# Tile copies on another queue, statistics in pieces, and router logits from the rows before their norm

## The chip, the core and the metric

The kernel runs on one core of one Trainium2 chip. TensorE multiplies matrices and accumulates in PSUM banks of 128 x 512 fp32, VectorE, ScalarE and GpSimd work element by element on SBUF (VectorE and ScalarE on PSUM too), and SyncE and ScalarE issue DMAs from queues of their own. The metric is the device time of one execution in microseconds, the median of several.

## What is computed

256 tokens of 1024 features go through two blocks. The first has two layers, `x = norm(ALPHA*x + mix)` and `x = norm(ALPHA*x + experts(x))`; in layer 0 `mix` is a convolution module, in layer 1 differential attention. The second block (a state-space mixer beside stick-breaking attention, and a feed-forward) is not touched. What the change bears on:

```python
def conformer_conv(x, w_pw1, b_pw1, w_dw, b_dw, g, b, w_pw2, b_pw2):
    a, gate = jnp.split(x @ w_pw1 + b_pw1, 2, axis=-1)
    h = depthwise_conv_31(a * jax.nn.sigmoid(gate), w_dw) + b_dw
    return jax.nn.silu(layer_norm(h, g, b)) @ w_pw2 + b_pw2

def grouped_moe(x, router_w, router_bias, w_gate, w_up, w_down):
    aff = jax.nn.sigmoid(x @ router_w)              # 16 experts in 4 groups
    # best group by the two best of aff + router_bias, then its two best experts
    # gates: aff of the two, over their sum
    out = sum_e gates[:, e] * ((jax.nn.silu(x @ w_gate[e]) * (x @ w_up[e])) @ w_down[e])
```

## The kernel before

The program is written as one straight line; a scheduler orders the instructions of each engine by the program's order, as far as their inputs and buffers are ready by its own model, and puts in the waits. `keep_in_program_order` and `after` (L341) pin single instructions.

Weights come in units of 1 MB in a fixed order (`order`, L283) through rings of SBUF slots: ring1 and ring2 hold 11 units, ring3, ring5 and ring4 another 8 once the convolution's or the attention's buffers are given back. All units are issued from SyncE's queue (`issue`, L317), each when its slot is free. fp32 products are made of three fast ones: a weight half is split in a high part (ScalarE, L367) and a low part (GpSimd or VectorE, L376), and `mm3` (L379) multiplies high by high, low by high and high by low.

`phase_a` (L568) is layer 0's convolution module. For each of 8 tiles of 128 channels the first projection is done on TensorE, ScalarE takes the sigmoid of the gate (`sg`), and VectorE writes the product to `hp` (L650). Channels are then convolved over time with 31 taps. Tiles 0, 1 and 3 are convolved on VectorE, tap by tap into a PSUM bank (L614; `CONV_RUNS` says how many taps follow each gate, and the next gate is pinned behind them). The other five go to TensorE: `shifted` (L596) writes `hp` of a tile to DRAM (`hd`, L603), reads it back four times with a shift (`xq`, L605), and makes a banded weight on GpSimd (L599); `conv` (L618) does 64 matmuls. Two convolutions are called between projections (tiles 5 and 6), three behind them, then `turn` (L626) transposes the result back to tokens by features in four banks, and `normalize` (L423) takes mean and variance (L429) and writes `n`. After silu the second projection `pw2` (`proj_q`, L698) runs over four units; in the last unit the four results (two token blocks by two halves of the features) are finished one after the other, and `done` adds each to the residual `res` (L689).

Then comes the routing, the same in both layers: `norm_rows` (L443) normalizes the residual rows in place; `moe` (L723) copies them as the high part `xnh` (ScalarE, L735), `to_fm` (L446) transposes them to features by tokens, VectorE and ScalarE apply gain and bias (L742, L744), 8 small matmuls in four column groups give the logits `lg` (L749), two more sum the groups (L754), and ScalarE takes the sigmoid `affs` (L756). VectorE makes the low part `xnl` (L759). `route` (L941) sorts on VectorE with some twenty small operations: `sel` (L945), ranks, masks, positions (by TensorE, L959), gates. `gather` (L777) then picks each expert's rows with one-hot matmuls over `xnh` and `xnl` (`px`, L787 and L790), and the experts begin. `warm` (L356) puts matmuls of no use on TensorE where it would stand idle; `W` counts them.

In attention `bias` (L1102) reads each head pair's bias from `vecd`, a DRAM table that holds a row of 384 values 128 times per head, so that one access pattern with a stride of 383 gives the diagonal form.

## Time and profile before

| | us |
|---|---|
| median of three runs (1165.78 to 1167.7) | 1167.34 |
| the profiled execution | 1166.63 |
| its span, first to last instruction | 1164.9 |

| stretch of the span, us | what runs |
|---|---|
| 0 to 89 | projections and convolutions of layer 0 |
| 89 to 119 | norm, silu, second projection |
| 119 to 139 | norm, routing and gather of layer 0 |
| 139 to 346 | experts of layer 0 |
| 346 to 469 | attention |
| 469 to 490 | norm, routing and gather of layer 1 |
| 490 to 697 | experts of layer 1 |
| 697 to 1165 | second block |

A row of a timeline gives the start in us from the span's start, the duration (of several instructions together, x their number), engine, line, operation, output<-inputs, shape, and in brackets how long the engine sat idle before and what ended that. PE is TensorE, DVE VectorE, ACT ScalarE, POOL GpSimd, SPq and ACTq the issuing queues of SyncE and ScalarE. A wait is put down to what came last by the profile. The clock is the mean share of TensorE's full clock that was granted.

### The profile page before, as it was taken

Reading aid. Unit: us, or ns where it says so; the run is one execution under the profiler, and the core shown is the slowest. Engines: PE = TensorE matmul, PEld = TensorE weight load, DVE = VectorE, ACT = ScalarE, POOL = GpSimd, SP = SyncE. Lnnn points to the kernel's source line nnn. Section 1 sums busy time; section 2 is a strip of 40 time slices with the busy share of each in tenths; the row PEclk is TensorE's granted clock in tenths of the full one; section 3 lists DMA queues with packets and bytes.
Section 4 is the critical chain, followed back from the end, with each engine's and each line's share of the span. In section 5 each row is a group of like instructions: output and inputs, shape, how many; then the busy total and the mean of one; then the engine's idle time right before and its main releaser. Section 6 shows DMA issues by size and latency. Waiting matters only on the chain.

```text
span 1164.9 us, 18257 instructions
## 1 busy us (share of the span) xinstructions
PE 1112.4 (95%) x7235; PEld 790.8 (68%) x7235; DVE 631.8 (54%) x1259; ACT 455.3 (39%) x798; POOL 308.1 (26%) x187
## 2 busy tenths in 40 slices
PE   9879989999999998989999999999999999999996
PEld 7857434444337997434344337989999988999996
DVE  6936721232227766721233227866988858665555
ACT  4314311011216665311011116555677566444443
POOL 5922000000003432000000005552324574444443
PEclk9989999999999999999999999999999999999998
DMA  9989489999999645599999993443323452554551
GB/s 358 308 260 403 152 364 418 420 419 421 419 415 415 238 161 218 240 372 387 419 419 421 419 418 106 161 155 118 128 92 109 173 208 73 217 181 167 196 199 55
DMA packets 53215, 315.11 MB, mean 271 GB/s; under 512 B 7111, under 2 KB 13312, under 8 KB 17024
## 3 DMA queue, kind: packets, MB, share of 16 engines
q1 hardware_dynamic: 49016, 309.02, 68.3%
q10 hardware_dynamic: 4104, 4.82, 1.3%
q8 instruction: 60, 0.98, 0.3%
q14 instruction: 35, 0.29, 0.1%
HBM read 312.01 MB, written 3.39 MB: 271 GB/s over the span
## 4 chain that ended last, share of the span: by engine, by line
PE 41%; DVE 9%; ACT 3%; DMA 1%; issue 1%; POOL 0%; ACTq 0%; DVEq 0%; POOLq 0%; SPq 0%
PE up L382 4%; PE up L383 4%; PE py L812 4%; PE up L381 4%; PE pu L812 4%; PE pg L812 3%; DVE E L1548 2%; PE pdn L383 2%; PE pdn L382 2%; PE pdn L381 2%; PE dwin L381 1%; PE dwin L382 1%; PE dwin L383 1%; DVE dwin L1342 1%; PE dwout L383 1%; PE dwout L382 1%
## 5 line engine op out<-in xcount | busy, mean ns | idle before, releaser
L812 PE MATMUL pu<-u_moe,xe 128*64 128x512 f32 x256 | 114.6, 600 | 4.7 <-PEq L991 4.7
L812 PE MATMUL py<-u_moe,hT 128*64 128x512 f32 x256 | 114.0, 596 | 1.4 <-DMA u_moe<-in_moe 0.8
L813 PE MATMUL pu<-u_moe,xe 128*64 128x512 f32 x256 | 114.7, 600 | 0.0
L813 PE MATMUL py<-u_moe,hT 128*64 128x512 f32 x256 | 113.6, 596 | 0.0
L812 PE MATMUL pg<-u_moe,xe 128*64 128x512 f32 x256 | 113.4, 593 | 0.0
L813 PE MATMUL pg<-u_moe,xe 128*64 128x512 f32 x256 | 113.0, 593 | 0.0
L881 DVE TENSOR_TENSOR h<-h,pu 128x512 f32<-128x512 f32 x16 | 11.0, 688 | 184.3 <-PE pu L813 171.6
L381 PE MATMUL dwin<-xih,wh 128*128 128x272 f32 (+1 forms) x352 | 104.8, 298 | 1.1 <-DVE xih L1288 1.1
L382 PE MATMUL dwin<-xil,wh 128*128 128x272 f32 (+1 forms) x352 | 102.1, 290 | 1.1 <-DVE xil L1289 1.1
L382 PE MATMUL up<-fxl,wh 128*128 128x258 f32 (+1 forms) x352 | 100.5, 285 | 1.6 <-DVE fxl L1729 1.6
L383 PE MATMUL dwin<-xih,wl 128*128 128x272 f32 (+1 forms) x352 | 101.5, 288 | 0.0
L381 PE MATMUL up<-fxh,wh 128*128 128x258 f32 (+1 forms) x352 | 100.4, 285 | 0.8 <-ACT fxh L1728 0.8
L383 PE MATMUL up<-fxh,wl 128*128 128x258 f32 (+1 forms) x352 | 100.4, 285 | 0.0
L376 POOL TENSOR_TENSOR wl<-u_win,wh 128x1024 fp32r<-128x1024 f32 x25 | 60.3, 2412 | 62.6 <-ACT wh L367 59.9
L916 DVE SCALAR_TENSOR_TENSOR yl<-py,gc,yh 128x512 fp32r<-128x512 f32 x32 | 24.0, 751 | 94.7 <-ACT yh L915 93.7
L812 PEld LDWEIGHTS pu<-u_moe,xe 128*64 128x64 f32 x256 | 35.1, 138 | 59.2 <-issue 58.0
L812 PEld LDWEIGHTS py<-u_moe,hT 128*64 128x64 f32 x256 | 33.4, 137 | 59.9 <-issue 56.0
L812 PEld LDWEIGHTS pg<-u_moe,xe 128*64 128x64 f32 x256 | 34.6, 137 | 54.7 <-issue 53.6
L376 POOL TENSOR_TENSOR wl<-u_wup,wh 128x1024 fp32r<-128x1024 f32 x22 | 52.8, 2401 | 64.7 <-ACT wh L367 64.7
L382 PEld LDWEIGHTS up<-fxl,wh 128*128 128x128 f32 x352 | 67.7, 192 | 2.5 <-DVE fxl L1729 1.8
L381 PEld LDWEIGHTS up<-fxh,wh 128*128 128x128 f32 x352 | 67.6, 192 | 2.0 <-ACT fxh L1728 1.3
L382 PEld LDWEIGHTS dwin<-xil,wh 128*128 128x128 f32 x352 | 67.0, 190 | 2.0 <-DVE xil L1289 1.9
(526 smaller groups left out, 3025.6 us busy)
## 6 DMA issues: line engine op xcount, KB each, us to landing
u_moe<-in_moe SPq DMA_DIRECT2D x192, 1024.0 KB, 18.6
u_win<-in_win SPq DMA_DIRECT2D x22, 1024.0 KB, 4.9
u_wup<-in_wup SPq DMA_DIRECT2D x22, 1024.0 KB, 5.3
u_pw<-in_pw SPq DMA_DIRECT2D x11, 1024.0 KB, 11.6
u_wdown<-in_wdown SPq DMA_DIRECT2D x11, 1024.0 KB, 4.9
u_wout<-in_wout SPq DMA_DIRECT2D x8, 1024.0 KB, 4.9
u_wk<-in_wk SPq DMA_DIRECT2D x4, 1024.0 KB, 15.8
u_wq<-in_wq SPq DMA_DIRECT2D x4, 1024.0 KB, 16.2
```

The costliest lines, as they stand in the source:

```text
L376: eng.tensor_tensor(l, w, h.bitcast(F32), ALU.subtract)
L381: mm(ps, lh, rh, start=first, stop=False)
L382: mm(ps, lh, rl, start=False, stop=False)
L383: mm(ps, ll, rh, start=False, stop=last)
L812: nc.tensor.matmul(ps[0:64], a, ra, start=first, stop=last)
L813: self.upped = nc.tensor.matmul(ps[64:128], b, rb, start=first, stop=last)
L881: nc.vector.tensor_tensor(h, h, pu, ALU.mult)
L916: nc.vector.scalar_tensor_tensor(yl[:, s], py[nh], gc, yh[:, s].bitcast(F32), op0=ALU.mult, op1=ALU.subtract)
L1342: nc.vector.scalar_tensor_tensor(pb, raw[:, k:k + L], wc(k), pb, op0=ALU.mult, op1=ALU.add)
L1548: nc.vector.tensor_scalar(E[:, q:q + w], a[:, i, q:q + w], nA[:, c, h:h + 1], 0.0, op0=ALU.add, op1=ALU.min)
```

## The change

In the convolution: `hd` is written from ScalarE's queue; there are four `xq` buffers for three; one convolution lies between projections (behind tile 6) and four behind them; the tiles are transposed in the order of `TURN`, in three goes between the convolutions, and the statistics are taken in four pieces per token block. `vecd` holds 32 copies for 128, made one projection earlier, and each bias load becomes four DMAs of 32 partitions.

In the routing: gain, bias and mean are taken out of the logits. With r = 1/std and m = mean of a row, `(x - m)*r*g @ w + b @ w` is `r*(x @ (g*w)) - m*r*(g @ w) + b @ w`. `router` makes `g*w` and the two constants of each expert early in stage A. `Head.done`, behind each finished quarter of the residual, adds it, takes its statistics, and transposes the quarter before it as it is, not normalized; ScalarE copies that to `xr`. `last` does the logits from `xr`, and `gates` applies r and m to the 16 logits of a row. The rows are normalized behind that (`rows`), one block on VectorE, one on GpSimd, and GpSimd makes the low part in four pieces.

```diff
-W = dict(start=16, a=16, l0=16, lg=9, pos=(4, 6), f0=22, f1=22, l1=18, mix=20)
+W = dict(start=16, a=13, head=(1, 2), lg=13, pos=(4, 6), f0=22, f1=22, mix=20)
+TURN = (0, 1, 2, 4, 5, 6, 3, 7)
+VCOPY = 32
+class Head:
+    def turn(self, tb, nh):
+        bank = self.net.bank(f"rt{self.l}{tb}{nh}")
+        s = slice(nh * 512, nh * 512 + 512)
+        for j in range(4):
+            self.nc.tensor.transpose(bank[:, j * P:(j + 1) * P], self.res[tb][:, (4 * nh + j) * P:(4 * nh + j + 1) * P], self.net.ident)
+        self.nc.scalar.activation(self.xr[tb][:, s], bank, AF.Copy)
+    def done(self, tb, nh, pp):
+        x = self.res[tb][:, nh * 512:nh * 512 + 512]
+        nc.vector.tensor_tensor(x, pp, x, ALU.add)
+        nc.vector.bn_stats(self.st[tb][:, nh], x)
+        if nh:
+            nc.vector.bn_aggr(self.mv[:, tb], self.st[tb])
+        if self.due:
+            self.turn(*self.due)
+        self.due = (tb, nh)
+    def last(self):
+        self.lg = net.bank(f"lg{l}")
+        self.logits(0, range(KT))
+        net.warm(W["head"][0])
+        self.turn(*self.due)
+        nc.vector.tensor_scalar(v, self.mv[:, :, 1], LN_EPS, None, op0=ALU.add)
+        self.r = net.rsqrt_act(v, [P, TB], f"l{l}")
+        nc.vector.scalar_tensor_tensor(self.nmr, self.mv[:, :, 0], -1.0, self.r, op0=ALU.mult, op1=ALU.mult)
+        self.logits(1, range(4))
+        net.warm(W["head"][1])
+        self.logits(1, range(4, KT))
+    def gates(self, b1):
+        nc.scalar.activation(lgs, self.lg[:, :T], AF.Copy)
+        net.preload(AF.Sigmoid)
+        for tb in range(TB):
+            nc.tensor.matmul(pa[:, tb * NE:(tb + 1) * NE], lgs[:, tb * P:(tb + 1) * P], net.col("groups", 0, NE), start=True, stop=True)
+        for tb in range(TB):
+            nc.vector.scalar_tensor_tensor(lin[:, tb], net.cd[:, l, 0], self.nmr[:, tb:tb + 1], net.cd[:, l, 1], op0=ALU.mult, op1=ALU.add)
+        for tb in range(TB):
+            self.lin = nc.vector.scalar_tensor_tensor(lin[:, tb], pa[:, tb * NE:(tb + 1) * NE], self.r[:, tb:tb + 1], lin[:, tb], op0=ALU.mult, op1=ALU.add)
+        nc.scalar.activation(aff, lin, AF.Sigmoid)
+    def rows(self, xnh, xnl):
+        for tb in range(TB):
+            i = (nc.gpsimd if tb else nc.vector).tensor_scalar(self.res[tb], self.res[tb], self.mv[:, tb, 0:1], self.r[:, tb:tb + 1], op0=ALU.subtract, op1=ALU.mult)
+            if not tb:
+                self.net.after(i, self.lin)
+            self.net.tc.keep_in_program_order(nc.scalar.activation(xnh[tb], self.res[tb], AF.Copy))
+        for h in range(2):
+            s = slice(512 * h, 512 * h + 512)
+            for tb in range(TB):
+                i = nc.gpsimd.tensor_tensor(xnl[tb][:, s], self.res[tb][:, s], xnh[tb][:, s].bitcast(F32), ALU.subtract)
...
-        self.vecd = self.dram.tile([NH, P, 384], F32, name="vecd")
+        self.vecd = self.dram.tile([NH, VCOPY, 384], F32, name="vecd")
...
-        self.pe3 = self.pool(early, "pae3", 3)
+        self.pe3 = self.pool(early, "pae3", 4)
...
-            self.load(hd, hp[:, j])
+            nc.scalar.dma_start(hd, hp[:, j])
...
+        def moments(c):
+            for tb in range(TB):
+                nc.vector.bn_stats(stats[tb][:, c], halves[tb][c // 2][:, c % 2 * 256:c % 2 * 256 + 256])
...
-            if j in (0, 1, 4):
+            if j in (0, 1, 3):
                 next(rel_bias, None)
-            if j in (5, 6):
+            if j in (2, 3, 5):
+                next(router, None)
+            if j == 6:
                 conv()
...
-        while conv_in:
-            conv()
-        for i in range(2):
-            turn(i)
+        conv()
+        conv()
+        turn(0, 1, 2, 3)
+        conv()
+        turn(4, 5)
+        for c in range(3):
+            moments(c)
+        conv()
+        turn(6, 7)
+        moments(3)
...
+            for i in range(P // VCOPY):
+                nc.scalar.dma_start(bt[VCOPY * i:VCOPY * i + VCOPY], ...)
```

## Rows read from the trace of the kernel before

**Rows 1.** The page: busy time, share of the span and instructions of each engine.
```profile
PE 1112.4 (95%) x7235; PEld 790.8 (68%) x7235; DVE 631.8 (54%) x1259; ACT 455.3 (39%) x798; POOL 308.1 (26%) x187
```
**Rows 2.** Windows: length, busy PE PEld DVE ACT POOL, clock, DMA share, GB/s.
```profile
79.10:83.50 4.40, 0.00 (x0) 0.00 (x0) 0.00 (x0) 0.44 (x1) 0.00 (x0) 1.00 1.07 242
83.60:88.90 5.30, 5.30 (x65) 2.94 (x66) 0.00 (x0) 0.00 (x0) 0.00 (x0) 0.68 1.01 418
...
130.00:140.00 10.00, 8.98 (x55) 5.51 (x55) 7.67 (x29) 3.32 (x5) 0.00 (x0) 1.00 0.01 3
140.00:160.00 20.00, 19.25 (x92) 6.84 (x90) 5.20 (x11) 1.09 (x3) 0.00 (x0) 1.00 0.89 354
```
**Rows 3.** Waits of TensorE from 50 to 90 us: total, times, longest.
```profile
PE cv L623 <- DMA xq<-hd: 10.5, 3, 4.8
```
**Rows 4.** Waits of SyncE's queue over the whole span.
```profile
SPq L275 <- DMA hd<-hp: 25.5, 5, 10.7
```
**Rows 5.** Timeline of SyncE's queue: start, duration, what is issued.
```profile
64.73 0.38 SPq L275 DMA_DIRECT2D hd<-hp  x1
...
72.55 0.34 SPq L275 DMA_DIRECT2D hd<-hp  x1
...
75.44 1.75 SPq L275 DMA_DIRECT2D xq<-hd  x4
```
**Rows 6.** Timeline of TensorE: last convolutions, then the routing of layer 0.
```profile
59.33 3.25 PE L623 MATMUL cv<-xq,band 128*32 128x256 f32 x29 [4.78 <-DMA xq<-hd]
...
75.35 3.66 PE L623 MATMUL cv<-xq,band 128*32 128x256 f32 x64 [1.15 <-DMA xq<-hd]
83.56 5.33 PE L623 MATMUL cv<-xq,band 128*32 128x256 f32 x64 [4.55 <-DMA xq<-hd]
...
118.58 0.39 PE L383 MATMUL pw<-wh,sl 128*128 128x512 f32 x1
...
122.73 2.16 PE L452 MATMUL fm_x1T<-cst_m,res 128*128 128x128 f32 x16 [0.26 <-DVE res L440]
...
133.80 0.36 PE L787 MATMUL px<-S,nh 128*128 128x256 f32 x1
```
**Rows 7.** Timeline of VectorE: taps, the first norm, the routing of layer 0.
```profile
57.46 9.41 DVE L614 SCALAR_TENSOR_TENSOR conv<-hp,cols_a,conv 128x256 f32<-128x256 f32 x18
...
72.03 0.48 DVE L650 SCALAR_TENSOR_TENSOR hp<-pw,cols_a,sg 128x256 f32<-128x256 f32 x1 [2.00 <-ACT sg L649]
...
92.29 0.17 DVE L432 TENSOR_SCALAR v_a<-mv_a 128x2 f32<-128x2 f32 x1
...
129.91 0.19 DVE L945 TENSOR_TENSOR sel<-affs,row_router_b 128x32 f32<-128x32 f32 x1 [1.94 <-ACT affs L756]
```
**Rows 8.** DMAs that write or read tile xq: issue to landing.
```profile
DMA to landing us min/median/max: 3.5/6.1/10.2
```
**Rows 9.** Groups by line and form, 118 to 131 us: busy, mean ns, idle before.
```profile
L759 DVE TENSOR_TENSOR nl<-res,nh 128x1024 fp32r<-128x1024 f32 x2 | 2.4, 1216 | 0.0
...
L735 ACT ACTIVATE nh<-res 128x1024 fp32r<-128x1024 f32 x2 | 2.0, 1040 | 0.0
...
L440 DVE TENSOR_SCALAR res<-res,mv_l,y_l 128x512 f32<-128x512 f32 x2 | 1.0, 542 | 0.0
```
**Rows 10.** Groups of GpSimd over the whole span: the nearest prices.
```profile
L1818 POOL TENSOR_TENSOR o<-o,hm 128x512 f32<-128x512 f32 x3 | 3.7, 1260 | 9.0 <-DVE o L1817 9.0
...
L762 POOL CAST idg<-cst_m 128x256 fp32r<-128x256 f32 x2 | 0.8, 396 | 17.7 <-PE wo L383 10.3 <-PE pw L383 7.4
```
**Rows 11.** Timelines of GpSimd and VectorE in attention: two small operations in a row.
```profile
404.59 2.43 POOL L376 TENSOR_TENSOR wl<-u_wv,wh 128x1024 fp32r<-128x1024 f32 x1 [7.03 <-ACT wh L367]
...
404.61 2.43 DVE L419 SCALAR_TENSOR_TENSOR t_sub<-t_sub,ss 128x4 f32<-128x4 f32 x1
407.07 0.16 DVE L420 SCALAR_TENSOR_TENSOR y_sub<-t_sub,y_sub 128x4 f32<-128x4 f32 x1
```
**Rows 12.** Timeline of ScalarE's queue in attention.
```profile
401.96 0.38 ACTq L1104 DMA_DIRECT2D bt<-vecd  x1
```

More of the change, by code (lines that the diff above doesn't have):

```diff
@@ L426, in normalize @@
         for tb in range(TB):
-            st = self.tiny.tile([P, 2, 6], F32, tag="bnst", name=f"st_{name}{tb}")
-            for i in range(2):
-                nc.vector.bn_stats(st[:, i], src[tb][i])
+            if stats:
+                st = stats[tb]
+            else:
+                st = self.tiny.tile([P, 2, 6], F32, tag="bnst", name=f"st_{name}{tb}")
+                for i in range(2):
+                    nc.vector.bn_stats(st[:, i], src[tb][i])
             nc.vector.bn_aggr(mv[:, tb], st)
@@ L485, in build @@
             c3 = ExitStack()
-            xs = self.phase_a(late, early, c3) if "A" in phases else self.skip("n1", c3)
-            for i in range(TB):
-                self.dump(f"n1{i}", xs[i])
+            xs, head = self.phase_a(late, early, c3)
             rows = lambda l: self.rows.get(l) or self.mix_rows(l)
             if "B" in phases:
-                xs, src = self.moe(0, xs, "mix_g0", "mix_b0", ["ring4", "ring5", "ring3"], rows(0))
+                xs, src = self.moe(0, xs, head, "mix_g0", "mix_b0", ["ring4", "ring5", "ring3"], rows(0))
             else:
@@ L498, in build @@
             self.retire = {}
-            xs = self.attention(xs, c3) if "C" in phases else self.skip("n3", c3)
-            for i in range(TB):
-                self.dump(f"n3{i}", xs[i])
+            xs, head = self.attention(xs, c3)
             if "D" in phases:
-                xs, src = self.moe(1, xs, "mix_g1", "mix_b1", ["ring4", "ring5", "ring3", "ring2"], rows(1))
+                xs, src = self.moe(1, xs, head, "mix_g1", "mix_b1", ["ring4", "ring5", "ring3", "ring2"], rows(1))
             else:
@@ L555, in rel_bias, with router @@
         yield
-        self.vecd = self.dram.tile([NH, P, 384], F32, name="vecd")
-        self.load(self.vecd, bass.AP(tensor=vecs.tensor, offset=vecs.offset, ap=[[384, NH], [0, P], [1, 384]]))
+        self.vecd = self.dram.tile([NH, VCOPY, 384], F32, name="vecd")
+        self.load(self.vecd, bass.AP(tensor=vecs.tensor, offset=vecs.offset, ap=[[384, NH], [0, VCOPY], [1, 384]]))
+    def router(self, pool, pin):
+        nc = self.nc
+        cols = self.held["cols_m"]
+        at = COL_AT["mix_g0"][1]
+        affine = cols[:, at:at + 8 * KT].rearrange("p (l c k) -> p l c k", l=DEPTH, c=4)
+        self.gw = self.yy.tile([P, DEPTH, (KT + 1) * NE], F32, name="gw")
+        nc.gpsimd.memset(self.gw[:, :, KT * NE:], 0.0)
+        for l in range(DEPTH):
+            self.after(nc.gpsimd.tensor_tensor(self.gw[:, l, :KT * NE].rearrange("p (k e) -> p k e", e=NE), self.col("router_w", 0, KT * NE).rearrange("p (k e) -> p k e", e=NE),
+                                    affine[:, l, 0].unsqueeze(2).to_broadcast([P, KT, NE]), ALU.mult), pin())
+        yield
+        pc = self.bank("cd")
+        for k in range(KT):
+            r = slice(32 * (k % 4), 32 * (k % 4) + 32)
+            nc.tensor.matmul(pc[r, :4], self.col("router_w", NE * k, 32), affine[:, :, 0:2, k], start=k < 4, stop=k >= 4)
+        part = pool.tile([P, 4], F32, name="cd_part")
+        nc.scalar.activation(part, pc[:, :4], AF.Copy)
+        yield
+        both = pool.tile([P, 384], F32, tag="rb_oh", name="ones_m")
+        ones, spread = both[:, :P], both[:, P:P + 4 * NE].rearrange("p (c e) -> p c e", c=4)
+        self.after(nc.gpsimd.memset(ones, 1.0), pin())
+        nc.gpsimd.tensor_tensor(spread, self.col("groups", 0, NE).unsqueeze(1).to_broadcast([P, 4, NE]), part.unsqueeze(2).to_broadcast([P, 4, NE]), ALU.mult)
+        pd = self.bank("cds")
+        nc.tensor.matmul(pd[:, :4 * NE], ones, spread.rearrange("p c e -> p (c e)"), start=True, stop=True)
+        self.cd = self.yy.tile([P, DEPTH, 2, NE], F32, name="cd")
+        nc.scalar.activation(self.cd.rearrange("p l c e -> p (l c e)"), pd[:, :4 * NE], AF.Copy)
     def open_a(self, late, early):
@@ L634, in phase_a @@
         rel_bias = self.rel_bias(e1)
+        router = self.router(e1, lambda: glu)
         res = [self.act.tile([P, D], F32, tag=f"xacc{tb}", name=f"res{tb}") for tb in range(TB)]
@@ L666, in phase_a @@
         self.preload("natural_log_exp_and_others")
-        while conv_in:
-            conv()
-        for i in range(2):
-            turn(i)
+        conv()
[8 more added lines that the diff above has]
+        moments(3)
         self.dump("convy", y)
         self.warm(W["a"])
-        self.normalize(halves, n, "a", AF.Silu)
+        self.normalize(halves, n, "a", AF.Silu, stats)
         early.close()
@@ L721, in mix_rows, with moe @@
         return [self.row(f"mix_{c}{l}", self.yy, t, late) for c, t in (("g", "yh"), ("b", "yl"))]
[L723 removed]
+    def moe(self, l, n, head, gname, bname, last_rings, rows):
         nc = self.nc
```

88 lines of the change are left out of this document (46 added, 42 removed).

## The prediction

> **What bounds the kernel now.** First the page: TensorE is busy 95% of the span and the other engines at most 68% [rows 1]. So time can only be saved where TensorE waits or works slowly, or where it runs for nothing. The second thing to look for is what the DMA does in those places, because the two expert stages load 96 MB each and a start of the experts that comes earlier is worth nothing if their weights do not come earlier too.
>
> The windows show both. In front of the first expert stage the DMA stands still: it moves 3 GB/s from 130 to 140 us, while TensorE is in the routing, and 354 GB/s from 140 to 160 us [rows 2]; in front of the second the same stretch is there again (two in all). The rings are full there, and the next slot comes free when the first experts have used a unit. So an expert stage that begins x us earlier restarts the stream x us earlier, and what is saved up to the end of a routing goes through to the end of the kernel one to one, as long as x is less than the standing time (10 us or more). What follows behind the experts is not touched by the change.
>
> The change touches three stretches that are in series with everything else:
> - the depthwise convolution and the norm behind it. TensorE waits 10.5 us in three pieces for the shifted copies xq [rows 3], and because it stood idle from 79.1 to 83.5 us it does the last convolution at a mean clock of 0.68 [rows 2], that is between the two levels of 1.2 and 2.4 GHz: 5.33 us where the same 64 matmuls took 3.66 us [rows 6];
> - the routing of layer 0, from the last matmul of the projection (its start at 118.58 plus 0.39 is 118.97 us; I call this end E) to the first matmul of the gather at 133.80 us: 14.8 us [rows 6];
> - the same routing in layer 1.
>
> **Stage A, part by part.** A tile's way is: VectorE writes hp, SyncE copies it to DRAM (hd), waits for the landing, loads xq from it, TensorE convolves. SyncE does this in order, and it waited 25.5 us for five landings of hd, once 10.7 us [rows 4]. So the copy of tile 6 went out at 64.73 us [rows 5], though VectorE had finished that tile's hp before it began the taps at 57.46 us [rows 7]: over 7 us lost in the queue alone. The change issues hd from ScalarE's queue, and each xq can be loaded as soon as its own hd has landed.
>
> The second thing is the order on TensorE. The last gate (hp of tile 7) was ready at 72.03 us because TensorE came to tile 7's projection only after the wait for tile 4's copy. Now only one convolution lies between projections. Tile 6's projection ended at 59.33 - 4.78 = 54.5 us, where the wait for tile 4 began [rows 6], with one convolution (3.66 us) ahead of it that now follows it, so tile 7's projection (5.9 us) runs from about 54.5 to 60.4 us, and its gate waits only for the 18 taps that precede it in VectorE's order: 57.46 + 9.41 + 0.48 = 67.4 us [rows 7], 5.1 us earlier than now.
>
> From there: ScalarE issues hd in 0.4 us, landing 2.5 us (72.55 to 75.44 now, less the issue [rows 5]), so xq of tile 7 is issued at 70.3 us. Now it took from 75.44 to 83.56 us to arrive [rows 5, 6], 8.1 us; landing times of all twenty pieces lie between 3.5 and 10.2 us with 6.1 in the middle [rows 8]. I take 7.2 us, between 6.1 and 8.1: 77.5 us. TensorE is there before: 60.4 + three convolutions of 3.7 + twelve transposes at 0.135 (16 took 2.16 us [rows 6]) + 1 us for the new router matmuls = 74.1 us. It idles 3.4 us, so I leave the last convolution at its slow 5.33 us: end at 82.9 us. Behind it come ScalarE's copy (0.5), the last 4 transposes (0.7 with latency), two short statistics (0.8) and the rest (0.6): v_a at 85.5 us against 92.29 us [rows 7]. **Gain 6.8 us, I say 7.** Bounds: with xq in 4.8 us (3.5 plus the other issues) and full clock 10.9 us; with 11.5 us for xq 2.6 us. The smaller DRAM copy vecd (0.4 MB for 1.5 MB) is inside these bounds.
>
> What pays: hd on ScalarE's queue makes ScalarE wait for VectorE's gate. Behind it in order stand the weight split of tile 7 and the sigmoid of the gate. For tile 6 this can hold ScalarE up to 57.5 us, and tile 7's projection would end at 66 us rather than 60.4, still below 67.4; then TensorE reaches the last convolution at 80 us and the gain is about 6, within the bounds. GpSimd gets about 1.2 us of small router work; it has slack once the bands of later tiles wait for their buffers.
>
> **The routing, per layer.** Removed from the path: the write of the normalized rows, 16 transposes behind it (2.16 us [rows 6]), the affine copies. Added ahead of E: three groups of four transposes on TensorE between projection matmuls, 12 x 0.135 = 1.6 us, uncovered. So E moves to E' = E + 1.6. From E', with durations of the same operations in layer 0: addition and statistics to the variance 1.9 us, then Ln behind the last copy of the turned sums (0.3 late), Ln, Exp and three small operations: r at E' + 3.3. Meanwhile the logits: last turn at E' + 1.0 to 1.5, ScalarE's copy to 2.3, last logits to 2.9, copy to 3.3, sums over groups to E' + 3.9. So the scalars and the logits come out together, and VectorE can put them together (four small operations) by E' + 4.4 at the best.
>
> Then the new costs. GpSimd normalizes one row block at r, and this is a form that the trace doesn't have; the nearest is a cast of 256 columns in 396 ns, so 1.6 us for 1024, and above it the two-input 1024 columns in 2.43 us [rows 10, 11]. Does it hold VectorE up? In attention a VectorE operation on 128x4 that normally takes 0.16 us took 2.43 us, exactly as long as GpSimd's operation beside it [rows 11]. So I take 1.2 us for this: the four operations end at E' + 5.6. VectorE's own row block follows (two halves of 542 ns [rows 9], 1.1 us) and only then sel: E' + 6.75. From sel to the gather it is 133.80 - 129.91 = 3.9 us as now [rows 6, 7]. Sum: E + 1.6 + 6.75 + 3.9 = E + 12.25 for E + 14.8 now, **gain 2.6 us**.
>
> Last, the low halves xnl. They lay on VectorE, 2.4 us behind the affine copies while the logits were under way [rows 9], and move to GpSimd, four operations on 128x512 at 1.26 us [rows 10]. They can start 1.15 us behind sel (ScalarE's copy xnh, 1.04 us [rows 9]), so they lie beside the sorting operations on VectorE, which wait for nothing else. If none is held the cost is 0; if each of the four holds one operation, 4 x 1.0 = 4.0 us. I take 1.4 us: the reductions and the operations that read PSUM need not be held, and of the small operations in attention only those that began under a running GpSimd operation were. **Gain 1.2 us per layer**, bounds +3.8 (nothing held, VectorE's combination at 4.4) and -2.2 (2.43 for 1.6, and 4.0).
>
> The Trainium skill has a rule on this, in "SBUF — State Buffer", section "Who interferes with whom": a VectorE instruction with two SBUF inputs and a GpSimd instruction that reads SBUF share one port pair under an exclusive lock, and the second one blocks for the whole of the first. By it the low halves would take the whole 4.0 us and a layer would lose 1.4 us instead of gaining 1.2; rows 11 agree with it, the other operations of this chain were never seen beside GpSimd.
>
> **Attention.** The bias loads become 16 issues for 4. One issue is 0.38 us of ScalarE's queue [rows 12]; three more, at two places inside softmax, are 1.2 us each time. TensorE has projections to do beside softmax, so I count 0.3 us in all; uncovered it is 2.4 us.
>
> **Sum.** The profiled execution took 1166.63 us (span 1164.9), 0.7 us below the median of the three, within their spread. 1166.6 - 7.0 - 2 x 1.2 + 0.3 = **1157.5 us**.
>
> **Rivals.**
> - Nothing is held: GpSimd's operations fall into gaps of VectorE's chain. For it: half of the sorting chain are reductions and PSUM reads. 1166.6 - 7 - 7.6 + 0.3 = 1152.3 us.
> - The copies don't come earlier: hd leaves from another queue but over the same DMA engines, which are full (share 1.07 from 79.1 to 83.5 us [rows 2]), and xq stays behind 1 MB loads in SyncE's queue. Then only the lower bound of stage A, 2.6 us: 1161.9 us. "DMA: Bandwidth & Descriptors" of the Trainium skill, section "Issuing engines are not separate DMA queues", speaks for this one: another issuing engine saves only the issue time. By that alone stage A would gain next to nothing and the sum would be about 1164 us; the wait of SyncE for landings [rows 4] speaks against it.
> - Slower: the lock in each routing. GpSimd's 2.43 us and all four low halves stand between VectorE's operations (E + 18.1, a loss of 3.3 us), and TensorE, which has then nothing to do for over 6 us, drops to the lower level as at 83.6 us [rows 2] and loses about 1.9 us on the gather: 5.2 us per layer. 1166.6 - 7 + 10.4 + 0.3 = 1170.3 us. It decides as soon as a layer loses more than half of what stage A gains, 3.5 us.
>
> **How the numbers follow.** Forecast 0.48, nothing held 0.22, copies no earlier 0.16, slower 0.14. A measurement here tells about 0.2%, 2.3 us, from no change. Faster than that are the first three cases except the lower edge of the third: 0.80; the same 0.08; slower 0.12. The range leaves out the slower case and a little of the lower bounds: 1148 to 1166 us.
>
> **What would show it.** Stage A: the waits of TensorE for xq fall from 10.5 to about 4 us, the last gate lies near 67 us, v_a near 85.5 us. Routing: E to the gather in about 13.5 us, with VectorE's sorting operations at 0.2 to 0.3 us (not held) or single ones above 1 us beside a GpSimd operation (held). The DMA standstill is shorter by what the routing comes earlier. Wrong would be: hd waiting on ScalarE until its splits are late, or a new wait of TensorE in attention for splits behind the bias loads.

## The result, and the profile after

The changed kernel took 1180.22 us, median of four runs (1178.17 to 1182.76); the kernel before, beside it, 1166.56 us (1163.36 to 1167.7). The ratio is 1.0123, 95% interval 1.0091 to 1.0154: it is 1.2% slower, and outside the range of the prediction. Each median below stands with its ratio to the kernel before, run on the same chip.

The first view is a table of milestones, read from the timelines: the start of the row named, in us. E is the end of the last matmul of `pw2`, px the first matmul of the gather, pg the first expert's first matmul.

| | before | after | later by | of which in this stretch |
|---|---|---|---|---|
| last gate (hp of tile 7) | 72.03 | 72.72 | 0.7 | 0.7 |
| v_a | 92.29 | 100.30 | 8.0 | 7.3 |
| E, layer 0 | 118.97 | 127.88 | 8.9 | 0.9 |
| first px | 133.80 | 141.34 | 7.5 | -1.4 |
| pg | 137.77 | 146.39 | 8.6 | 1.1 |
| gather of the second group of experts | 180.7 | 192.6 | 11.9 | 3.3 |
| last pg of layer 0 | 326.40 | 339.72 | 13.3 | 1.4 |
| warm matmuls before attention | 347.5 | 362.5 | 15.0 | 1.7 |
| attention's last projection wo, start | 439.58 | 454.06 | 14.5 | -0.5 |
| wo, end | 468.79 | 485.79 | 17.0 | 2.5 |
| first px, layer 1 | 483.9 | 499.2 | 15.3 | -1.7 |
| pg, layer 1 | 487.90 | 504.59 | 16.7 | 1.4 |
| last pg of layer 1 | 678.63 | 696.84 | 18.2 | 1.5 |
| end of the span | 1164.86 | 1180.98 | 16.1 | -2.1 |

Half of the loss is there at v_a. The second block, which the change does not touch, took 465.6 to 468.6 us in the thirteen traces of this study (from the end of the last `py` of layer 1, the down projection of the experts, to the end of the span); the -2.1 in the last line, and 2 or 3 us of any single span, lie within that. The work itself is nearly what it was; the row of the page that answers to [rows 1]:

```profile
PE 1112.2 (94%) x7255; PEld 794.2 (67%) x7262; DVE 631.2 (53%) x1257; ACT 454.2 (38%) x796; POOL 325.7 (28%) x202
```

TensorE is busy for the same 1112 us, so 16 us of waiting have been added. GpSimd is the engine that has more to do, 17.6 us.

**Stage A.** Windows of after (length, busy PE PEld DVE ACT POOL, clock, DMA share, GB/s), beside [rows 2]:

```profile
50.00:56.00 6.00, 5.67 (x27) 5.67 (x28) 5.61 (x12) 0.22 (x1) 0.27 (x2) 0.53 0.55 151
...
60.00:80.00 20.00, 13.04 (x172) 9.66 (x168) 11.61 (x23) 5.03 (x7) 8.57 (x4) 0.90 0.26 82
...
66.00:70.00 4.00, 4.00 (x53) 3.27 (x55) 2.91 (x5) 2.37 (x3) 0.43 (x1) 1.00 0.00 2
```

Before, the DMA share from 60 to 80 us was 0.84 at 224 GB/s; now it is 0.26, and next to nothing (2 GB/s) moves from 66 to 70 us. And TensorE works at a granted clock of 0.53, near its lower level of 1.2 GHz, from 50 to 56 us. Who waited for what, TensorE from 30 to 104 us, beside [rows 3]:

```profile
PE cv L727 <- DMA xq<-hd: 10.2, 3, 7.0
PE cds L659 <- POOL ones_m L656: 4.8, 1, 4.8
```

and SyncE's queue, from 54 to 76 us, beside [rows 4]:

```profile
SPq L356 <- DMA hd<-hp: 20.6, 2, 12.1
```

The waits for xq have not become smaller (10.2 us for 10.5), a wait of 4.8 us for a constant of the new router has come in, and SyncE, which no longer writes hd, waits for the landing of hd longer than before, 12.1 us at once. The timelines of both queues and GpSimd, beside [rows 5]; first SyncE:

```profile
62.62 13.67 SPq L356 DMA_DIRECT2D xq<-hd  x4
...
76.81 2.65 SPq L356 DMA_DIRECT2D xq<-hd  x4
...
80.04 5.77 SPq L356 DMA_DIRECT2D xq<-hd  x4
```

ScalarE's queue:

```profile
60.87 0.33 ACTq L707 DMA_DIRECT2D hd<-hp  x1
...
73.22 0.33 ACTq L707 DMA_DIRECT2D hd<-hp  x1
```

The four pieces of one xq (tile 5, the first row) take 13.67 us to issue: the first goes out at 62.62 us, the second not before 75.04 us. Those are the two moments at which the copies of tile 6 (issued 60.87) and tile 7 (73.22) land, 1.7 and 1.8 us behind their issue. Tile 5's loads need neither. Why they wait stands in the program as it was built. It has eight completion counters for the DMAs of both queues, dealt out in turn in the order in which the scheduler planned the DMAs, and a DMA is issued only when the one that held its counter before it has landed:

```
planned  queue    transfer        counter  held before by
34       ScalarE  hd of tile 6    1        xq, tile 2
35       ScalarE  hd of tile 7    2        hd of tile 4
37..40   SyncE    xq, tile 4      4 to 7   (four others)
42       SyncE    xq, tile 5, 1   1        hd of tile 6
43       SyncE    xq, tile 5, 2   2        hd of tile 7
```

The scheduler's model expects the copies of tiles 6 and 7 early, so it dealt them counters ahead of loads that on the chip could go first. Once hd stands on another queue, nothing but this counter ties the two.

**Routing of layer 0.** Timelines, beside [rows 6, 7, 9 to 11]; TensorE, with the two other waits that are new:

```profile
50.33 0.69 PE L659 MATMUL cds<-ones_m 128*128 128x64 f32 x2 [4.81 <-POOL ones_m L656]
...
138.98 0.17 PE L1059 MATMUL pos<-maskb,cst_mb 128*128 128x16 bf16 x1 [4.13 <-DVE maskb L1056]
...
141.69 0.41 PE L890 MATMUL px<-S,nl 128*128 128x256 f32 x1
144.57 0.28 PE L890 MATMUL px<-S,nl 128*128 128x256 f32 x1
...
192.61 0.58 PE L887 MATMUL px<-S,nh 128*128 128x256 f32 x1 [4.00 <-DVE S L873]
```

VectorE:

```profile
100.30 0.17 DVE L516 TENSOR_SCALAR v_a<-mv_a 128x2 f32<-128x2 f32 x1
...
131.42 1.18 DVE L288 SCALAR_TENSOR_TENSOR lin<-cd,nmr_l 128x16 f32<-128x16 f32 x2
...
135.27 1.22 DVE L1035 TENSOR_TENSOR rkd_g<-gs 128x32 f32<-128x32 f32 x1
136.52 1.19 DVE L1036 TENSOR_TENSOR rkd_g<-rkd_g,cst_m 128x32 f32<-128x32 f32 x1
137.97 0.97 DVE L1056 SCALAR_TENSOR_TENSOR maskb<-rk_g,top 128x32 bf16<-128x32 f32 x1
138.86 1.30 DVE L1056 SCALAR_TENSOR_TENSOR mask<-rk_g,top 128x32 f32<-128x32 f32 x1
```

GpSimd:

```profile
45.49 4.63 POOL L457 TENSOR_TENSOR wl<-u_pw,wh 128x1024 fp32r<-128x1024 f32 x2
50.08 0.19 POOL L656 MEMSET ones_m<- 128x128 f32 x1
...
131.38 3.79 POOL L298 TENSOR_SCALAR res<-res,mv_l,y_l 128x1024 f32<-128x1024 f32 x1 [11.78 <-DVE nmr_l L273]
135.18 4.93 POOL L306 TENSOR_TENSOR nl<-res,nh 128x512 fp32r<-128x512 f32 x4
```

Small VectorE operations beside GpSimd's low halves take about as long as one of those, 1.23 us, instead of 0.15 to 0.3 us; `lin` is held beside the normalization. The five rows hold some 4.7 us in excess. The memset of 0.19 us at 50.08 stands behind two weight splits of 4.63 us: that is TensorE's wait of 4.81 us, and the clock of 0.53 came behind it.

**Experts: the branch.** The gather of the second group waits 4.0 us (1.9 us in layer 1) for `S`, which VectorE makes behind the branch for overflowing experts. The program puts that branch on every engine, SyncE passes it only in its queue's order, and the scheduler had put 34 weight units ahead of it instead of 30.

**Experts: the bias loads.** SyncE's queue, from 290 to 350 us; before, then after:

```profile
SPq L317 <- DMA bt<-vecd: 12.3, 1, 12.3
```
```profile
SPq L398 <- DMA bt<-vecd: 12.6, 1, 12.6
```

The waits are alike, their places are not. Before, all expert units of the layer were out (the last at 326.67 us) when SyncE waited for the landing of a bias load (`bt`) of attention; the wait ended at 341.8 us and held a weight of attention. Now each bias load is four DMAs, so eight of them and not two hold counters here; SyncE waits until 343.8 us, and only then do the last four expert units go out. From 336 to 346 us the DMA moves 183 GB/s.

### The profile page after: what moved, and what is told of

Same layout as the page of the kernel before. It is cut to its first block, busy times and chain, and to the rows that moved or that the text cites. A ratio compares the mean times of both kernels' runs of the same rounds, so it can differ in the third digit from the quotient of the medians.

```text
span 1181.0 us, 18322 instructions
## 1 busy us (share of the span) xinstructions
PE 1112.2 (94%) x7255; PEld 794.2 (67%) x7262; DVE 631.2 (53%) x1257; ACT 454.2 (38%) x796; POOL 325.7 (28%) x202
## 4 chain that ended last, share of the span: by engine, by line
PE 37%; DVE 7%; ACT 3%; DMA 3%; POOL 1%; issue 1%; ACTq 0%; DVEq 0%; POOLq 0%; SPq 0%
PE up L463 4%; PE up L464 4%; PE up L462 4%; PE py L912 3%; PE pg L912 2%; PE pu L912 2%; PE pdn L464 2%; PE pdn L463 2%; DMA u_moe<-in_moe 2%; PE pdn L462 2%; DVE E L1649 2%; PE dwin L462 2%; PE dwin L463 2%; PE dwin L464 2%; PE dwout L464 1%
## 5 line engine op out<-in xcount | busy, mean ns | idle before, releaser
L912 PE MATMUL pu<-u_moe,xe 128*64 128x512 f32 x256 | 114.6, 600 | 3.7 <-PEq L1091 2.1
L912 PE MATMUL py<-u_moe,hT 128*64 128x512 f32 x256 | 114.3, 596 | 2.8 <-DMA u_moe<-in_moe 2.2
L913 PE MATMUL pu<-u_moe,xe 128*64 128x512 f32 x256 | 114.7, 600 | 0.0
L913 PE MATMUL py<-u_moe,hT 128*64 128x512 f32 x256 | 113.9, 596 | 0.0
L912 PE MATMUL pg<-u_moe,xe 128*64 128x512 f32 x256 | 113.4, 593 | 0.0
L913 PE MATMUL pg<-u_moe,xe 128*64 128x512 f32 x256 | 113.0, 593 | 0.0
L912 PEld LDWEIGHTS py<-u_moe,hT 128*64 128x64 f32 x256 | 33.3, 137 | 61.7 <-issue 56.1
L912 PEld LDWEIGHTS pu<-u_moe,xe 128*64 128x64 f32 x256 | 35.1, 139 | 58.3 <-issue 57.1
L912 PEld LDWEIGHTS pg<-u_moe,xe 128*64 128x64 f32 x256 | 34.6, 137 | 54.7 <-issue 54.1
L464 PEld LDWEIGHTS up<-fxh,wl 128*128 128x128 f32 x352 | 67.8, 192 | 0.0
```

Source lines behind the costliest of these rows:

```text
L464: mm(ps, ll, rh, start=False, stop=last)
L912: nc.tensor.matmul(ps[0:64], a, ra, start=first, stop=last)
L913: self.upped = nc.tensor.matmul(ps[64:128], b, rb, start=first, stop=last)
```

## The experiments

The theory after the traces: three separate losses, (1) the ones behind the splits and the counters in stage A, (2) the lock on VectorE in the routing, (3) the branch behind more loads. The rivals: that one of them alone explains the rest, and that what the copies gain or lose lies in the queue that issues them.

**The ones without their pin.** The memset was pinned behind the gate of tile 5.

```diff
-        self.after(nc.gpsimd.memset(ones, 1.0), pin())
+        nc.gpsimd.memset(ones, 1.0)
```

> The changed kernel with one pin removed: the memset of the router's matrix of ones is no longer tied behind the gate of tile 5, so it stands early on GpSimd and not behind two weight splits at 50.1 us. Theory A (two delays in series in the convolution: TensorE waits 4.8 us for this memset and then works at a clock of 0.53 for 6 us, and the last gate and everything behind it is late by that): the wait is gone, the last gate moves from 72.7 to about 68 us, the third shifted copy (issued at 75.0 us) goes with it, v_a comes at about 95.6 instead of 100.3 us, and the time is about 4.7 us lower, 1175.5 us. Rival B (the memset wait is covered, the copies alone set the end of the convolution): v_a stays near 100 us and the time at 1180.

1179.88 us, ratio 1.0107 (1.006 to 1.0153). A miss: not the pin alone holds it. Its buffer is shared with the one-hot rows of the bias, so the memset, now early in GpSimd's order, waits for those and holds the splits behind it. Waits of GpSimd and TensorE in this kernel:

```profile
POOL ones_m L656 <- ACT sg L762: 4.8, 1, 4.8
```
```profile
PE pw L464 <- POOL wl L457: 2.9, 1, 2.9
```

The wait was moved, not removed, and the last gate came at 73.75 us.

**The copies' counters.** On top of that edit, each copy is planned behind the loads of the tile two before it, so that no xq shares a counter with a copy that comes later.

```diff
+            i = nc.scalar.dma_start(hd, hp[:, j])
+            self.copy = i
+            if len(self.shift) >= 2:
+                self.after(i, self.shift[-2])
...
+            self.shift.append(last)
...
+            if self.copy:
+                self.after(sig, self.copy)
```

> The kernel of e1 with, in addition, the planner told to place the copy hd of a tile behind the last load xq of the tile two before it, and the sigmoid of the next tile behind that copy; no instruction waits for this at run time. It changes the order in which transfers get their completion counters: the program has eight, handed round in the planner's order, and a transfer is issued only when the one that had its counter before it has landed. In the changed kernel two of the four loads of xq for tile 5 share counters with the hd copies of tiles 6 and 7 that the planner put ahead of them, and SyncE waits for those landings at 62.6 and 75.0 us. Theory A (this false wait is what delays the copies): the loads for tile 5 go out at about 53 to 55 us, those of tile 7 near 71 us, v_a comes at 85 to 88 us and the time is about 1164 to 1167 us. Rival B (the loads are late because hd lands late over full DMA engines): they stay behind 70 us, and the time is that of e1.

1171.58 us, 1.0042 (1.0023 to 1.0062), 8.3 us less than without this edit; v_a at 89.41 us, 8.7 us earlier. SyncE's queue in this kernel, the last three xq:

```profile
55.70 1.73 SPq L358 DMA_DIRECT2D xq<-hd  x4
...
67.23 1.73 SPq L358 DMA_DIRECT2D xq<-hd  x4
...
77.11 1.73 SPq L358 DMA_DIRECT2D xq<-hd  x4
```

Four pieces go out in 1.73 us each time. All that the edit changes is the place of the copies, and of the sigmoids behind them, in the planned order, and with it the counters: 8.7 us at v_a are theirs, and they come through to the end.

**The ones earlier.** The memset and its buffer moved into an earlier piece of the router's work, behind the gate of tile 3.

```diff
+        both = pool.tile([P, 384], F32, tag="rb_oh", name="ones_m")
+        self.after(nc.gpsimd.memset(ones, 1.0), pin())
         part = pool.tile([P, 4], F32, name="cd_part")
         nc.scalar.activation(part, pc[:, :4], AF.Copy)
         yield
```

> The changed kernel with the memset of the router's ones tied behind the gate of tile 3 instead of tile 5. In e1 the memset, free of its pin, stood so early that GpSimd waited 4.8 us for the buffer that it shares with the bias table, and everything behind it was late by that; here the buffer is free and the result is wanted ten us later. Theory A (the memset is a delay of its own): TensorE's wait of 4.8 us and its half clock behind it are gone, GpSimd gets no new wait, gate 6 comes at 57 to 58 us instead of 60.4 and gate 7 at 69 to 70 instead of 72.7; xq for tile 5, still bound to the landing of tile 7's copy, follows, v_a comes at about 97 us and the time is 3 us lower, 1177 us. Rival B (VectorE's taps and the other splits set the gates): gate 7 stays near 72.7 us and the time at 1180.

1177.9 us, 1.0102 (1.0075 to 1.013). The last gate comes at 69.0 us, 3.7 us earlier, v_a at 96.23, 4.1 us earlier. The median fell by 2.3 us, which the spread of these runs (1175.5 to 1185.1) doesn't tell from none. TensorE now waits 12.4 us for xq, as the counters still hold those.

**Both.** The last two edits together.

> e5 and the counter order of e2 together: both delays of the convolution are out. Theory A (two delays in series, which e2 showed to be worth 8.7 us of v_a for the counters): v_a at 85 to 87 us, 3 us below e2's 89.4, and the time at about 1168 us; that is still no gain over the kernel before although v_a is 6 us earlier than there, because the routing and the branch take it back. Rival B (the convolution was the whole loss): 1160 us.

1172.07 us, 1.0028 (1.0002 to 1.0055); v_a at 90.05 us. A miss: the last gate is 4 us earlier than in the kernel with the counters alone, and v_a is not. Something else ends last now; the last experiment looks for it.

**The routing on VectorE.** The row block and the low halves that went to GpSimd go back.

```diff
-            i = (nc.gpsimd if tb else nc.vector).tensor_scalar(self.res[tb], ...)
+            i = nc.vector.tensor_scalar(self.res[tb], ...)
...
-                i = nc.gpsimd.tensor_tensor(xnl[tb][:, s], ...)
+                i = nc.vector.tensor_tensor(xnl[tb][:, s], ...)
```

> The changed kernel with GpSimd taken out of the routing: the normalization of row block 1 and the four low halves are done by VectorE. Theory A (while GpSimd runs one of these, a VectorE operation with two operands in SBUF is held until GpSimd is done): the five held operations, 0.97 to 1.30 us each in layer 0, go back to 0.15 to 0.3 us; VectorE gets 0.8 and 4 times about 0.62 us more, so the gather begins about 12.1 us behind the last projection matmul instead of 13.5, and the matmuls of the gather keep the short price. Gain 1 to 2.4 us per layer, 1175.5 to 1178 us. Rival B (the operations were long because they waited for something else): they stay at about 1 us and the added 3.3 us per layer make it slower, about 1187 us.

1174.44 us, 1.0061 (1.0032 to 1.0091), 5.8 us less than the changed kernel in two layers. VectorE in this kernel:

```profile
130.07 0.38 DVE L288 SCALAR_TENSOR_TENSOR lin<-cd,nmr_l 128x16 f32<-128x16 f32 x2
...
133.53 0.19 DVE L1035 TENSOR_TENSOR rkd_g<-gs 128x32 f32<-128x32 f32 x1
133.64 1.89 DVE L306 TENSOR_TENSOR nl<-res,nh 128x512 fp32r<-128x512 f32 x3
...
135.89 0.19 DVE L1056 SCALAR_TENSOR_TENSOR maskb<-rk_g,top 128x32 bf16<-128x32 f32 x1
```

Every operation that was held is back at 0.15 to 0.3 us, though VectorE does more work; E to px is 11.45 us for 13.46, and to `pg`, behind the gather, it is 15.8 us for 18.5 (in layer 1, from the end of `wo`, 16.3 for 18.8): 5.2 us in the two layers, which the time agrees with. VectorE makes the low halves between the small operations, at 0.63 us each, in half of GpSimd's time.

**Only the row block on VectorE.** The first of those two lines alone; one run.

> The changed kernel with only the normalization of row block 1 moved from GpSimd to VectorE; the four low halves stay on GpSimd. It splits what e4 did in one. Theory A (the price of GpSimd's normalization, 3.79 us, and the lock by the low halves are separate losses): VectorE's lin operation of 1.01 us goes back to 0.24, block 1 is there at about r + 2.4 us instead of r + 3.8, the low halves start 1 us or more earlier, still hold three or four of VectorE's operations for about 1 us each, and the gather begins about 12.5 us behind the last projection matmul, between the 13.5 of the changed kernel and the 11.5 of e4. Rival B (GpSimd's normalization is the whole loss): 11.5 us and no operation held.

1178.65 us, beside 1167.95 for the kernel before. `lin` is no longer held (0.23 us) and the gather starts 12.99 us behind E; the four later operations are held as before (1.01, 1.18, 0.96, 1.30 us) by the low halves. So of 2.0 us at px, 0.5 belong to the row block and 1.5 to the low halves.

**The branch earlier.** Loads are planned later around the branch, so that fewer of them stand ahead of it.

```diff
+                if p == 1:
+                    self.LAG = LAGS[1] + 4
...
+                    self.LAG = LAGS[1]
+                    self.flush(self.LAG)
```

> The changed kernel with four weight loads held back in each expert stage until the branch that guards the overflow is behind: 30 units are issued ahead of the branch as in the kernel before, where the changed kernel issues 34. Theory A (at the branch SyncE waits for all its loads to land, and with four more of them VectorE's selection of the second group comes after TensorE has run out of work): the wait of TensorE for S, 4.0 us in layer 0 and 1.9 us in layer 1, goes, and the time falls by 3.2 and 1.6 us, to about 1175.5 us. Rival B (the wait for S comes from the late stream of weights, which began late because of the convolution): it stays, and the time stays at 1180.

1179.61 us, 1.0105 (1.0057 to 1.0153): in time inconclusive, 0.6 us less. The wait for `S` is gone, and from the first pg to the last pg the two stages became 2.8 and 4.4 us shorter. The tails of the stages (from the last pg on) gave back 1.0 and 1.2 us; attention and the second block, which this edit leaves alone, came out 2.1 and 1.3 us longer in this one trace. Groups of TensorE in the experts of layer 0, this kernel (busy, mean ns, idle before):

```profile
L912 PE MATMUL pu<-u_moe,xe 128*64 128x512 f32 x128 | 58.2, 607 | 2.4 <-PEq L1095 2.4
L912 PE MATMUL py<-u_moe,hT 128*64 128x512 f32 x128 | 57.4, 596 | 3.4 <-DMA u_moe<-in_moe 3.1 <-ACT hT L996 0.3
```

In the changed kernel `py` waited 2.2 us for weights and `pu` took 593 ns; now it is 3.1 us and 607 ns. The matmuls of L912 and L913 run side by side in pairs, so the slower `pu` costs once 128 times 14 ns, 1.7 us by the busy time.

**Stage A and routing, then all three.** The edits of stage A with the routing on VectorE; then with the branch too.

> e6 with the routing of e4 (no GpSimd in it). Theory A (the mended convolution and the freed routing add up): e6 less the 5.8 us that e4 gained, about 1162 us, with the first gather near 123 us and the stretch from the last projection matmul to the gather at 11.5 us as in e4. Rival B (what the routing gains is taken back by the stream of weights, which then is late): the same stretches, but waits of TensorE for weights, and no more than 1 us below e6.

1163.62 us, 0.9969 (0.9945 to 0.9993).

> e7 with the branch of e3, 30 units ahead of it. Theory A: the wait for S at the second group, 2 to 4 us per layer, is gone and the time is 3 to 5 us below e7, about 1158 us. Rival B (as the time of e3 suggests, which fell by 0.6 us only although its expert stages were 2.8 and 4.4 us shorter: the stages behind take it back): the expert stages are shorter, and the time is within 2 us of e7.

1161.61 us, 0.9951 (0.992 to 0.9981): faster than the changed kernel and than the one before. The branch brings 2.0 us between the medians, with runs from 1158.8 to 1166.4 us without it and from 1157.9 to 1165.0 with it: not clear of noise. v_a:

```profile
87.78 0.17 DVE L518 TENSOR_SCALAR v_a<-mv_a 128x2 f32<-128x2 f32 x1
```

The gather starts at 126.8 us, 7.0 us earlier than before, but the span is only 4.9 us shorter.

**The copies on SyncE again.** The same kernel with hd on SyncE's queue and without the planning of the copies, which it no longer needs; everything else of the change is kept.

```diff
-            i = nc.scalar.dma_start(hd, hp[:, j])
+            self.load(hd, hp[:, j])
```

> e8 with the copies hd back on SyncE's queue, as in the kernel before; the order of the convolutions, the statistics in pieces, the routing on VectorE and the early branch stay. It asks what the first half of the change's name is worth when nothing stands in its way. Theory A (the prediction's: SyncE's order costs 7 us for tile 6): hd of tile 6 goes out 3 us or more later than in e8, the last copies are later by that, v_a comes at 91 us or later instead of 87.8, and the time is 3 to 5 us above e8. Rival B (the landing, not the issue, sets the time, and the new order of the convolutions is the gain): v_a within 1.5 us of e8 and the time too.

1162.74 us, 0.9961 (0.994 to 0.9981), and

```profile
87.98 0.17 DVE L516 TENSOR_SCALAR v_a<-mv_a 128x2 f32<-128x2 f32 x1
```

v_a is 0.2 us later, and hd of tile 6 goes out at 57.29 us, from ScalarE's queue at 61.20. Kernels of this study with the same stage A differ at v_a by 2.3 and 2.4 us between traces (87.78 to 90.05, 98.34 to 100.76), so no gain of ScalarE's queue for the copies shows here; one of 2 us or less at v_a could not be told. The 4.3 us at v_a against the kernel before come from what else the change does in stage A (order of the convolutions, fourth buffer, statistics in pieces); I did not take these apart. The rule of the Trainium skill that the prediction named (page "DMA: Bandwidth & Descriptors", section "Issuing engines are not separate DMA queues") agrees with that; it doesn't speak of counters.

**Weights behind the copies.** The kernel with all three edits, and from tile 5 on the expert weights are planned behind the copies and their loads.

```diff
+            self.LAG = LAGS[0] if j < 5 else 8
...
+        self.LAG = LAGS[0]
+        self.flush(self.LAG)
```

> e8 with the first three expert weight loads behind unit 0 (3 MB) issued behind the copies of tile 7 and not between the copies. In e8 the copies hd of tiles 6 and 7 took 5.5 and 7.5 us to land beside such loads, in the changed kernel, where the DMA stood idle, 1.7 and 1.8 us. Theory A (they compete for the DMA engines): both land in 2 to 3 us, xq of tile 7 goes out at about 72 us instead of 77 and v_a comes at about 83.5 instead of 87.8 us; but the 3 MB are missing in the rings when the experts begin, the standstill of the DMA of 8.5 us is gone and TensorE waits for weights at the end of the first expert stage, so the time changes by less than half of that, 1159 to 1162 us. Rival B (standing time is still left over, as I counted in the prediction): the whole 4 us arrive, 1157.5 us.

1160.85 us, 0.9935 (0.991 to 0.9959), the lowest median of the study; the interval overlaps that of the kernel with all three edits. The copies of tiles 6 and 7 land 1.8 us behind their issue; with 1 MB loads under way it had been 5.5 and 7.5 us. v_a:

```profile
85.35 0.17 DVE L518 TENSOR_SCALAR v_a<-mv_a 128x2 f32<-128x2 f32 x1
```

Its TensorE no longer waits for xq; it waits for ScalarE instead:

```profile
71.60 0.98 PE L744 MATMUL ty<-cst_m,y 128*128 128x128 f32 x5 [3.30 <-ACT y L734]
72.51 5.08 PE L733 MATMUL cv<-xq,band 128*32 128x256 f32 x64
...
79.64 3.66 PE L733 MATMUL cv<-xq,band 128*32 128x256 f32 x64
```
```profile
69.42 0.33 ACTq L709 DMA_DIRECT2D hd<-hp  x1
...
71.08 0.84 ACT L734 ACTIVATE y<-cv,cols_a 128x256 f32<-128x256 f32 x2
```

The copies `y` of two finished convolutions stand behind the copy of tile 7 in ScalarE's order, which waits for VectorE's gate at 68.91 us.

2.4 us are gained at v_a and 2.2 at the gather; in the time it is 0.8, which these runs tell neither from none nor from 2.2. The trace tells more: at the warm matmuls before attention 0.5 us are left (345.5 for 346.1). Groups of TensorE in the experts of layer 0; first the kernel before:

```profile
L812 PE MATMUL py<-u_moe,hT 128*64 128x512 f32 x128 | 57.2, 596 | 1.1 <-DMA u_moe<-in_moe 0.8 <-ACT hT L892 0.3
...
L812 PE MATMUL pu<-u_moe,xe 128*64 128x512 f32 x128 | 56.5, 593 | 2.3 <-PEq L991 2.3
```

the kernel with all three edits:

```profile
L920 PE MATMUL pu<-u_moe,xe 128*64 128x512 f32 x128 | 57.9, 605 | 2.5 <-PEq L1103 2.5
L920 PE MATMUL py<-u_moe,hT 128*64 128x512 f32 x128 | 57.4, 596 | 3.8 <-DMA u_moe<-in_moe 3.5 <-ACT hT L1004 0.3
```

and this one:

```profile
L923 PE MATMUL py<-u_moe,hT 128*64 128x512 f32 x128 | 58.9, 611 | 4.1 <-DMA u_moe<-in_moe 3.8 <-ACT hT L1007 0.3
...
L923 PE MATMUL pu<-u_moe,xe 128*64 128x512 f32 x128 | 56.7, 593 | 3.7 <-PEq L1106 2.2 <-DMA u_moe<-in_moe 1.5
```

From the first pg to the warm matmuls the kernel before takes 209.7 us, these two 215.0 and 216.7. With all three edits TensorE is idle for 2.9 us more in this stretch (2.7 of it `py` waiting for weights) and busy for 2.4 us more (1.4 of it the slower `pu`, 605 for 593 ns); with the weights behind the copies it is 4.3 us of waits and 2.6 us of work (1.7 of it the slower `py`). So the experts begin 6.7 and 9.0 us earlier, and 5.2 and 7.0 us of it go into the stage.

Why the weights are late stands in SyncE's queue, with all three edits from 300 to 330 us:

```profile
SPq L400 <- DMA u_moe<-in_moe: 16.2, 3, 12.0
SPq L400 <- DMA bt<-vecd: 10.2, 1, 10.2
```

and in ScalarE's:

```profile
323.63 4.26 ACTq L1217 DMA_DIRECT2D bt<-vecd  x8
```

It is the counters once more, this time those of the bias loads. SyncE waits 10.2 us, to 327.1 us, for one of them to land, and then sends the last four expert units of the layer within 1.4 us. The first lands at 332.83 and the third at 339.09 us, and two of the waits of `py` end there, at 333.0 and 339.2 us. Windows from 318 to 330 us, the kernel before and this one:

```profile
318.00:330.00 12.00, 12.00 (x54) 4.33 (x52) 2.73 (x3) 2.71 (x4) 0.00 (x0) 1.00 1.01 417
```
```profile
318.00:330.00 12.00, 12.00 (x57) 3.94 (x51) 0.00 (x0) 1.88 (x2) 0.00 (x0) 1.00 0.85 319
```

98 GB/s less for 12 us is 1.2 MB, or 2.8 us at the full rate (an estimate from these two rows). With the weights behind the copies the wait is 11.5 us. No kernel here was run with the bias loads as they were, so what they cost in time is not measured.

## Why the prediction was wrong

**Stage A, the premise.** The step that failed is "each xq can be loaded as soon as its own hd has landed". I forecast v_a at 85.5 us; it was 100.30. The counters account for 8.7 us of the miss, and the ones for 4.1 (in one pair of traces each, with the spread of 2.4 us at v_a named above). Each was measured with the other still there, and their sum need not be exact. When the counters, the ones and the weights in the copies' way are all mended, the routing's and the branch's edits being in the same kernel, the last gate is at 68.9 us (forecast 67.4), the last xq is issued at 71.3 (70.3) and v_a is at 85.35 us (85.5). So the premise was false, and the size of the gain behind it could be had. That v_a agrees to 0.2 us is luck in part, for TensorE came there another way. It waited for no xq (forecast 3.4 us) and did the last convolution in 3.66 us (forecast 5.33); instead it waited 3.30 us for ScalarE's `y`, and the convolution behind that wait took 5.08 us. That ScalarE's order would have a price I had seen for the splits and the sigmoid, not for `y`. I had read SyncE's waits for hd [rows 4] as the price of one queue's order. They showed only that SyncE waits; with the rest of the change in place, the kernel with the copies back on SyncE shows no cost of that order, and what it cost in the kernel before is not measured. A slip of reading: [rows 8] is not of all twenty pieces, the trace has a landing for ten of them.

**Stage A, the bounds.** I gave 2.6 us of gain as the lower end and as the rival "copies don't come earlier". Nothing in the trace excluded that they come later, and that was what happened. A lower end below zero would have been honest for a step with a new dependence between two queues.

**GpSimd's slack.** "It has slack" was argued from its share of the span [rows 1], not from the place: the memset of 0.19 us landed behind 4.63 us of splits, and TensorE stood still behind it. It is a short operation that costs by its place in the order.

**The routing.** The mechanism of the slower rival was right, and the sizes were off. GpSimd's normalization took 3.79 us where I took 1.6 and gave 2.43 as the upper bound; VectorE was held by 4.7 us in layer 0 where the sum had 1.2 + 1.4. From E I had 13.65 - 1.6 = 12.05 us to the gather, with E' taken as the new E; it was 13.46. The turns cost 0.9 us between v_a and E in layer 0 and 2.5 us in attention's projection in layer 1 (1.6 in the sum). Behind the wait of 4.13 us for `maskb` the gather ran at 0.41 us a matmul, later 0.28: the clock that the rival had counted with 1.9 us cost about 1.1. So from v_a to pg layer 0 lost 0.6 us instead of gaining 1.2, and from the start of wo to pg layer 1 lost 2.2 us. The rival had 5.2 us per layer. The rule of the Trainium skill (page "SBUF — State Buffer", section "Who interferes with whom") agrees with the rows and with the two kernels that take GpSimd's operations away; I had it before me and took a third of what it gave for the low halves.

**One to one.** "What is saved up to the end of a routing goes through to the end" failed. In the kernel with the weights behind the copies, 9.0 us at pg became 3.7 us at the end of the last `py` of layer 1 and 4.9 us of span; with all three edits 6.7 us became 2.2 and 4.9 us (what the span has more is the second block's own scatter). The standing time was not what failed. The DMA had stood still between 127.6 us, the landing of the last load ahead of the routing, and 141.4 us, the first issue behind it; with all three edits the stop is from 129.4 to 135.2 us, and with the weights behind the copies 3.6 us of it are left. The stream did restart earlier, by 6.2 and 8.5 us. But from the restart to the last landing of an expert unit before attention it then took at least 2.0 and 3.0 us longer than the 201.9 us before (the last unit's own landing isn't in these two traces), and in that time its last four units waited for the bias loads.

**The bias loads.** The forecast put 0.3 us on them, and looked for it in attention. There it holds: from the warm matmuls to wo 91.5 us for 92.1. The step that failed is that issuing them was all they cost: split in four they hold four times the counters, SyncE waits 10.2 to 12.6 us for them ahead of the last expert units, and `py` waits for weights. This the traces show; what it costs in time stays open.

**The experts.** The prediction held that only three stretches are touched. The branch was a fourth: the change moved loads around it in the scheduler's plan, and 4.0 and 1.9 us of waits came of that. The tail of the stage, with the bias loads, was a fifth.

## What to carry to other kernels

When a DMA moves to another queue, look at what else ties the queues: the order in which completion counters are dealt out, and what the scheduler believes of when each will be due. The same holds when one DMA becomes four: each piece takes a counter, and loads of another queue may wait for the last. A short operation given to an engine with slack costs by what stands ahead of it there, and beside small VectorE operations GpSimd's work is paid in whole GpSimd operations. Time saved ahead of a stage that streams its weights comes through only if the stream can end earlier too; look at what its last loads wait for before counting it one to one.

## What was not expected of the hardware

- GpSimd's normalization, 128x1024 with two scalars per partition, took 3.79 us; its two-input subtraction of four times 128x512 took 4.93 us for twice the columns.
- A 128-partition copy to DRAM landed 1.7 to 1.8 us behind its issue on an idle DMA, and 5.5 to 7.5 us behind it beside 1 MB loads.
- After much the same wait of TensorE at the branch, 2.31 us before, 2.48 us with all three edits and 2.47 us with the copies back on SyncE, the matmuls of `pu` took 593, 605 and 594 ns on the mean. What decides these runs don't show.
